# z projections of a mixer moved behind the Fourier inputs and kept in DRAM, with the Fourier branch beside the state steps

## Chip, cores and metric

The kernel runs on one core of one Trainium2 chip. The metric is the device time of one execution in microseconds, the median over several runs. The profile comes from one further execution, recorded by the hardware profiler; all times inside it count from its first instruction.

## What is computed

The program is a model of two blocks on 512 tokens of 1024 features. The first block has two layers of four attention branches with a feed-forward part. The second is one layer: modulation, a mixer, and a convolutional feed-forward part. The change is in the mixer. Cut to what matters, with `h` the modulated input:

```python
p = h @ w_in                                  # u, q, k, v, z and the gates, side by side
qkv = silu(dwconv1d(p[..., o1:o2], conv))     # three taps along the tokens; q and k to unit length
o, _, _ = bidir_gdn(q, k, v, beta, g, s_f, s_b)   # gated delta rule, forward scan + backward scan
y_f = fft2(u, axes=(tokens, group channels), norm='ortho').real @ w_f    # 4 groups of 128 features
y_d = rmsnorm_2(o, g_gdn) * silu(z)           # 4 heads of 128
y = concatenate([y_f, y_d]) @ w_out
x = x + gate * rmsnorm_2(y, g_post_mix)
```

One chunk of the delta rule, in each direction, needs the inverse of a triangular matrix I + A of its tokens (independent of the state), and then a step `v_new = u - w S`, `o = q S + attn v_new`, `S = S * decay + k^T v_new`.

## The kernel before

Values are held as pairs of float32r parts, high and low, and a product is three matmuls (L230 to L232). A weight block of 128x512 is loaded in fp32 by SP's DMA queue into `raw` (three buffers), cast by ScalarE to `whi` (L206), and its low part `wlo` is made by VectorE (L209) or GpSimd (L211), alternately; where `lo_pool` is true, always by GpSimd. A scheduler orders each engine's instructions, so that the order on an engine isn't that of the code.

The mixer's main part (the function that is printed below) works on four chunks of 128 tokens, four heads and two directions. In the order of the code:

- k, q and the gates; A of all chunks; the inverses of chunks 0 and 3, then of 1 and 2. An inverse begins with a substitution inside blocks of 16 tokens (L1174 shuffles, L1178 products, L1179 additions), whose second pair runs on VectorE with the products of one half (`own`) on GpSimd. It ends in `T` (L1189), which TensorE transposes (`tu`, L1200) and combines (`xp`, `up`).
- the Fourier inputs `us` (four projections of 128x512), q k^T for the steps (`gdn_attn`), the V projections with their convolution (`gdn_v`), and the Fourier matrix of each group, `Mg`.
- eight state steps, `gdn_step`: for each of four chunks both directions. On TensorE: `ks`, `qs`, `vp`, `av`, `sp`, 40 passes of 128x128. On VectorE: `S` and `r` from PSUM, `vd`, and `osum` or `ot`.
- `fourier`: first `between()`, the z projections (`proj_tm`, 192 matmuls of 128x256, eight weight blocks of `w2z`), then per group of features `V = u Mg` (16 matmuls) and 24 products `mm<-h,V` with the position matrix, and `yf` from them. z is evicted from PSUM by a tanh on ScalarE (`zt`, L1384) and one VectorE instruction (`zs`, L1385), which together give 2 silu(z); GpSimd multiplies it by the norm's gain (L1391).
- the gate of each chunk in the order 1, 0, 2, 3: the root mean square of `o` by small VectorE instructions on 128x4 elements (`ov`, `rq_i`, `rq_y`, `rq_t`, `of`), `oy` on VectorE (L1406), `oy` times `zs` on GpSimd (L1407), transposes `yt`, and the split `Yd`. Behind it the output projection `out_mix` and the sum of squares `ss` (L304).

The scheduler already places the 192 z matmuls partly between the steps: 150 of them stand in the steps and 42 behind them. The last `sp` of the steps ends near 2648.7 us.

Of the kernel before, what the change touches and what calls it, by code (L numbers as in the profile page):

```python
# [32 lines left out]
# ---------------------------------------------------------------- layout on the host  # L33
# [35 lines left out]
def pack(inp):  # L69
# [49 lines left out]
    # constants that depend on shapes alone  # L119
# [53 lines left out]
# ---------------------------------------------------------------- the program  # L173

class Prog:
# [12 lines left out]
    def side(self, shape, name):  # L188
        """Scratch of the work that runs beside a chain, which must not wait for the chain's own."""
        return self.wk.tile(shape, F32, name=name, tag="side", bufs=3)  # L190
# [5 lines left out]
    # ---- weights: fp32 as loaded -> an exact pair of float32r parts  # L196
# [17 lines left out]
    def blocks(self, src, nk, width=128, step=4):  # L214
        """Weights [128, nk * width], a pair of parts for each of the nk k-tiles."""
# [31 lines left out]
    # ---- 1/sqrt on the vector engine: shifted-exponent seed and three Newton steps  # L247
# [15 lines left out]
    # ---- 1/rms of each token over the features (on partitions), on every partition  # L263
# [24 lines left out]
    def rms_half(self, xs, scale=1.0 / D):  # L288
        """As rms, of half of the tokens."""
# [24 lines left out]
    def rms2(self, xs, gf):  # L314
        """For y = gain * x / rms(x): 1 / (rms(x) rms(y)) and 1 / rms(x) of each token, on every partition."""
# [55 lines left out]
    def setup_late(self):  # L371
        """Constants behind the first loads of x."""
# [17 lines left out]
    # ---- block 1  # L390
    def gain_split(self, xs, gcol):
        """Parts of x * gain, before the tokens' own factors 1 / rms are known."""
# [9 lines left out]
    def rms_row(self, xs, bank="t", tmp=None):  # L402
        """1 / rms of each token: along the free axis on every partition, and by token block."""
# [37 lines left out]
    def stack(self, t, z, i):  # L441
        """Parts of a head's 64 rows of z: rounded on its own rows of t, the rest on the other rows."""
        a, b = slice(i * 64, i * 64 + 64), slice(64 - i * 64, 128 - i * 64)
        self.nc.scalar.copy(t[a], z[a])
        self.nc.vector.tensor_sub(t[b], z[a], t[a])

    def score(self, s, q, k, a, stop):
        """q^T k in three products of parts; q stacked, k: parts of the keys on both halves of the rows."""
# [3 lines left out]
    def attn_head(self, h, score, add, diag, v, Y):  # L452
        """One causal head. v(b): parts of the values of key block b, side by side; Y: parts of the outputs."""
# [68 lines left out]
    def layer(self, l, xs):  # L522
# [23 lines left out]
        # -- indexer of branch B  # L546
# [21 lines left out]
        # -- branch A  # L568
# [31 lines left out]
        def pick(m, rounds=range(16)):  # L600
            """The 128 largest of each row become 0, the others NEG."""
# [48 lines left out]
        # -- branch B  # L650
# [16 lines left out]
        # -- branch C  # L667
# [28 lines left out]
        # -- branch D  # L696
# [20 lines left out]
        # -- out  # L717
# [194 lines left out]
    # ---- block 2  # L912
    def ada_steps(self):
        """Rows of the modulation's weights times silu(c), and for the first two also times silu(c_ctx)."""
# [67 lines left out]
    def gdn_k(self, G, H, n, between=None):  # L982
        """k: conv, silu, unit length; on tokens (G.ktm) and on features (G.kT)."""
# [73 lines left out]
    def gdn_gates(self, G, H, n):  # L1057
        """Beta, cumulated log decays and their exponentials (tokens on partitions)."""
# [37 lines left out]
    def gdn_a(self, G, cs):  # L1096
        """A of both directions of some chunks (before the triangle is cut out), and the decay."""
# [27 lines left out]
    def gdn_inv(self, G, cs, own=None):  # L1125
        """The inverse of I + A, transposed, columns of beta."""
# [16 lines left out]
    def tinv(self, G, As, own):  # L1143
        """Transposed inverses of I + A: by substitution within blocks of 16 tokens, then by pairs of blocks."""
        nc, n = self.nc, len(As)
        tl = lambda nm, shape: G.pool.tile(shape, F32, name=nm, tag=G.tags[nm][0], bufs=G.tags[nm][1])
        # the blocks' coefficients, columns in the order of the substitution
# [98 lines left out]
    def gdn_step(self, G, c, dr, S0, first):  # L1246
        """One chunk of one direction; S0: state before it (None: zero); returns the state after it."""
# [48 lines left out]
    def ctx_part(self, spool, mp):  # L1296
        """States of both directions after the context."""
# [29 lines left out]
    def mixer(self, xs, st, spool, mp):  # L1327
# [26 lines left out]
        for g in range(4):  # L1354
            nc.scalar.copy(us[g], self.proj(H, A["w2fm"][12 + g], S))
        self.lo_pool = False
# [293 lines left out]
```

## Time and profile before

| | before |
|---|---|
| median of 3 runs | 3150.69 us (3146.12 to 3153.24) |
| span of the profiled execution | 3146.6 us |
| mean granted TensorE clock | 0.976 |
| TensorE busy | 3005.7 us (96%) |
| VectorE busy | 2022.1 us (64%) |
| ScalarE busy | 1294.6 us (41%) |
| GpSimd busy | 853.4 us (27%) |

The span, from the first to the last instruction, is the only time shown for the profiled execution; the median lies 4.1 us above it. A busy share is an average over stages with different limits. What concerns the change lies between 2480 and 2720 us of the span.

### The profile page before, as it was taken

The page shows a single profiled execution, that of the slowest core. Times are in us where ns is not written, and L with a number is a line of the kernel's source. Part 1 is how long each engine was busy: PE and PEld are TensorE (multiplying, and loading weights), DVE is VectorE, ACT ScalarE, POOL GpSimd, SP SyncE. Part 2 cuts the span into 40 slices and gives each one's busy share as a digit, 9 for nine tenths or more (in the row PEclk, how much of TensorE's full clock was granted, in tenths as well). Part 3 has the DMA queues.
Part 4 walks back from the last instruction along what each step waited for, and adds up shares of the span by engine and source line. Part 5 has one row for each costly group of instructions (what it writes and reads, how often), then busy time and mean ns, then how long its engine had stood idle before and what let it go on. Part 6 is the DMA issues. An engine that isn't in the chain of part 4 may idle for free. (4 is left out here: it accounts for less than half of the span.)

```text
span 3146.6 us, 45203 instructions
## 1 busy us (share of the span) xinstructions
PE 3005.7 (96%) x16264; PEld 2496.3 (79%) x16264; DVE 2022.1 (64%) x4085; ACT 1294.6 (41%) x2601; POOL 853.4 (27%) x682
## 2 busy tenths in 40 slices
PE   8999999999999989999989999889999899899998
PEld 7767877788877868678877887778886689898997
DVE  5977264434978887874373436775466856785684
ACT  4355323334433333464233334533344533543332
POOL 2222324132222222113232332211221412422223
PEclk9999999999999989999999999999999999999998
DMA  3211312133344562112211233321332101323223
GB/s 124 70 37 44 101 57 89 44 111 131 111 151 161 173 190 81 38 41 74 94 61 61 93 123 97 102 61 65 96 91 96 60 23 53 116 67 93 98 85 110
DMA packets 152143, 280.97 MB, mean 89 GB/s; under 512 B 17520, under 2 KB 30192, under 8 KB 151792
## 3 DMA queue, kind: packets, MB, share of 16 engines
q1 hardware_dynamic: 146160, 266.93, 26.5%
q10 hardware_dynamic: 5472, 10.11, 1.0%
q8 instruction: 128, 2.10, 0.3%
q0 software_dynamic: 288, 1.05, 0.1%
q14 instruction: 95, 0.78, 0.1%
HBM read 271.74 MB, written 6.29 MB: 88 GB/s over the span
## 5 line engine op out<-in xcount | busy, mean ns | idle before, releaser
L211 POOL TENSOR_TENSOR wlo<-raw,whi 128x512 fp32r<-128x512 f32 (+3 forms) x446 | 597.6, 1341 | 1747.1 <-ACT whi L206 1586.5
L206 ACT CAST whi<-raw 128x512 fp32r<-128x512 f32 (+2 forms) x884 | 534.8, 608 | 998.1 <-PE mm L231 791.1
L230 PE MATMUL mm<-hhi,whi 128*128 128x512 f32 (+1 forms) x2520 | 927.5, 368 | 10.0 <-ACT whi L206 7.0
L232 PE MATMUL mm<-hhi,wlo 128*128 128x512 f32 (+2 forms) x2520 | 927.0, 368 | 4.6 <-DVE wlo L209 4.3
L231 PE MATMUL mm<-hlo,whi 128*128 128x512 f32 (+1 forms) x2520 | 923.2, 366 | 0.0
L230 PEld LDWEIGHTS mm<-hhi,whi 128*128 128x128 f32 x2520 | 478.2, 190 | 87.5 <-ACT whi L206 7.0
L232 PEld LDWEIGHTS mm<-hhi,wlo 128*128 128x128 f32 (+1 forms) x2520 | 477.8, 190 | 84.8 <-DVE wlo L209 6.0
L231 PEld LDWEIGHTS mm<-hlo,whi 128*128 128x128 f32 x2520 | 477.7, 190 | 77.5 <-issue 2.0
L209 DVE TENSOR_TENSOR wlo<-raw,whi 128x512 fp32r<-128x512 f32 (+3 forms) x438 | 326.5, 746 | 234.4 <-ACT whi L206 228.0
L230 PE MATMUL mm<-fhi,whi 128*128 128x512 f32 (+1 forms) x560 | 217.3, 389 | 17.4 <-ACT fhi L244 17.4
L231 PE MATMUL mm<-flo,whi 128*128 128x512 f32 (+1 forms) x560 | 217.5, 388 | 0.0
L232 PE MATMUL mm<-fhi,wlo 128*128 128x512 f32 (+1 forms) x560 | 217.0, 387 | 0.0
L230 PE MATMUL mm<-whi,hhi 128*128 128x256 f32 (+2 forms) x512 | 147.0, 287 | 6.5 <-ACT vM L562 5.6
L232 PE MATMUL mm<-yhi,wlo 128*128 128x512 f32 x384 | 152.0, 396 | 0.0
L230 PE MATMUL mm<-yhi,whi 128*128 128x512 f32 x384 | 151.9, 396 | 0.0
L231 PE MATMUL mm<-ylo,whi 128*128 128x512 f32 x384 | 151.2, 394 | 0.0
L231 PE MATMUL mm<-wlo,hhi 128*128 128x256 f32 (+2 forms) x512 | 147.1, 287 | 2.0 <-POOL wlo L211 2.0
L232 PE MATMUL mm<-whi,hlo 128*128 128x256 f32 (+2 forms) x512 | 146.4, 286 | 0.0
L230 PEld LDWEIGHTS mm<-fhi,whi 128*128 128x128 f32 x560 | 107.4, 192 | 41.1 <-ACT fhi L244 19.9
L739 DVE TENSOR_TENSOR mt<-mm,rrow 128x512 f32<-128x512 f32 x64 | 44.3, 692 | 134.8 <-PE mm L232 134.8
L1545 DVE SCALAR_TENSOR_TENSOR cv<-mm,cdwc,cv 128x441 f32<-128x441 f32 (+2 forms) x176 | 120.4, 692 | 10.6 <-PE mm L231 6.6
L231 PEld LDWEIGHTS mm<-flo,whi 128*128 128x128 f32 x560 | 107.8, 192 | 22.5 <-DVE flo L245 1.0
(513 smaller groups left out, 4922.1 us busy)
## 6 DMA issues: line engine op xcount, KB each, us to landing
raw<-wfm SPq DMA_DIRECT2D x240, 256.0 KB, 2.7
raw<-wup SPq DMA_DIRECT2D x176, 256.0 KB, 2.8
ada<-wada SPq DMA_DIRECT2D x48, 512.0 KB, 3.9
raw<-w2up SPq DMA_DIRECT2D x88, 256.0 KB, 2.8
raw<-wbr SPq DMA_DIRECT2D x64, 256.0 KB, 2.8
raw<-wdn SPq DMA_DIRECT2D x64, 256.0 KB, 2.7
raw<-w2fm SPq DMA_DIRECT2D x48, 256.0 KB, 2.8
raw<-w2dn SPq DMA_DIRECT2D x48, 256.0 KB, 2.7
```

The source lines that it names most:

```text
L206: nc.scalar.copy(hi[:, :n], raw[:, :n])
L209: nc.vector.tensor_sub(lo[:, :n], raw[:, :n], hi[:, :n])
L211: nc.gpsimd.tensor_sub(lo[:, :n], raw[:, :n], hi[:, :n])
L230: mm(out, a[0], b[0], start=first, stop=False)
L231: mm(out, a[0], b[1], start=False, stop=False)
L232: mm(out, a[1], b[0], start=False, stop=last)
L739: nc.vector.tensor_mul(t, g, self.row)
L1545: nc.vector.scalar_tensor_tensor(c[:, ro, co], p[:, ri, ci], w(a, b), c[:, ro, co], op0=OP.mult, op1=OP.add)
```

## The change

The z projections are called right behind the Fourier inputs, while `lo_pool` is true. They are evicted by a plain copy on ScalarE and stored to a DRAM tensor in eight parts of 128x256. Two loads of 128x1024 bring them back behind the steps, and tanh and the product of silu are then done from SBUF on 128x512. `fourier` no longer calls anything first. Its first two groups use the common PSUM banks alone (`both` false), so that they can stand beside the steps. The two directions of a step come in the order 1, 0.

```diff
+        def evz(j, p, i):
+            t = self.side([128, 256], "zt")
+            nc.scalar.copy(t, p)
+            nc.sync.dma_start(self.zspill[:, j, i * 256:i * 256 + 256], t)
+        for i in range(2):
+            self.proj_tm(H, A["w2z"][i], 256, lambda j, p: evz(j, p, i))
         self.lo_pool = False
...
         for i in range(4):
-            for dr in range(2):
+            for dr in (1, 0):
                 c = (3 - i) if dr else i
...
             z = mp.tile([128, 2, S], F32, name="zs", tag="T", bufs=2)
+            nc.sync.dma_start(z, self.zspill[:, 2 * i:2 * i + 2, :])
             zs += [z[:, 0, :], z[:, 1, :]]
-
-        def ev(j, p, i):
-            t = self.side([128, 256], "zt")
-            nc.scalar.activation(t, p, AF.Tanh, scale=0.5)
-            nc.vector.scalar_tensor_tensor(zs[j][:, i * 256:i * 256 + 256], t, 1.0, p, op0=OP.add, op1=OP.mult)
-        Y = self.fourier(us, Mg, mp, lambda: [self.proj_tm(H, A["w2z"][i], 256, lambda j, p: ev(j, p, i))
-                                          for i in range(2)])
+        Y = self.fourier(us, Mg, mp)
         gg = self.rows2[:, 16:144]
-        for j in range(4):
+        for j in (1, 0, 2, 3):
+            t = self.side([128, S], "zt")
+            nc.scalar.activation(t, zs[j], AF.Tanh, scale=0.5)
+            nc.vector.scalar_tensor_tensor(zs[j], t, 1.0, zs[j], op0=OP.add, op1=OP.mult)
             z4 = zs[j].rearrange("p (h e) -> p h e", h=4)
             nc.gpsimd.tensor_mul(z4, z4, gg[:, None, :].to_broadcast([128, 4, 128]))
...
-    def fourier(self, us, Mg, mp, between):
+    def fourier(self, us, Mg, mp):
         nc, ps, A = self.nc, self.ps, self.A
-        between()
-        self.both = True
...
         for g in range(4):
+            self.both = g > 1
...
+        P.zspill = nc.dram_tensor("zs", [128, 4, S], F32, kind="Internal").ap()
```

What this does to the order on the engines is shown at three places. The first is TensorE at the wait for `T` of the second pair of chunks. Before, V matmuls of 128x512 (output `mm`, inputs `hhi` and `hlo` from the left) stand ahead of it:

```order
L230 MATMUL mm_23104<-hhi_21529,whi_23113 128x512
L231 MATMUL mm_23104<-hlo_21530,whi_23113 128x512
L232 MATMUL mm_23104<-hhi_21529,wlo_23114 128x512
L1200 MATMUL tu_22351<-tri_98,T_22344 128x128 x4
L1200 MATMUL tu_22357<-tri_98,T_22344 128x128 x4
L1216 MATMUL xp_22376<-U_22350,A_21917 128x64
L1200 MATMUL tu_22364<-tri_98,T_22347 128x128 x4
```

Now the matmuls ahead of it are the z projections, of 128x256, weights from the left:

```order
L232 MATMUL mm_23139<-whi_23039,hlo_21512 128x256
L230 MATMUL mm_23139<-whi_23039,hhi_21511 128x256
L231 MATMUL mm_23139<-wlo_23040,hhi_21511 128x256
L1200 MATMUL tu_22351<-tri_98,T_22344 128x128 x4
L232 MATMUL mm_23139<-whi_23039,hlo_21512 128x256
L1200 MATMUL tu_22357<-tri_98,T_22344 128x128 x4
L230 MATMUL mm_23139<-whi_23045,hhi_21529 128x256
L1200 MATMUL tu_22364<-tri_98,T_22347 128x128 x4
```

The 48 V matmuls went behind `T`, and 83 z matmuls took the place; the other 109 z matmuls follow between `T` and the first step. The second place is TensorE in the seventh state step, from `qs` on. Before, z matmuls fill it:

```order
L232 MATMUL mm<-whi,hlo 128x256
L1263 MATMUL vp<-r,U 128x128
L230 MATMUL mm<-whi,hhi 128x256
L1263 MATMUL vp<-r,U 128x128
L231 MATMUL mm<-wlo,hhi 128x256
L1263 MATMUL vp<-r,U 128x128
L232 MATMUL mm<-whi,hlo 128x256
L1263 MATMUL vp<-r,U 128x128
L230 MATMUL mm<-whi,hhi 128x256
L231 MATMUL mm<-wlo,hhi 128x256
L232 MATMUL mm<-whi,hlo 128x256
L230 MATMUL mm<-whi,hhi 128x256
```

Now, from the seventh `ks` to the first products of the eighth step, one Fourier product and the `Mg,u` matmuls are left in the seventh, and none in the eighth:

```order
L1255 MATMUL ks<-S,kTx 128x128 x4
L1271 MATMUL qs<-S,qTx 128x128 x4
L232 MATMUL mm<-hhi,V 128x258
L1435 MATMUL mm<-Mg,u 128x128 x4
L1263 MATMUL vp<-r,U 128x128 x4
L1287 MATMUL sp<-vd,ktmx 128x128 x3
L1274 MATMUL av<-vn,attn 128x128 x4
L1287 MATMUL sp<-vd,ktmx 128x128
L1255 MATMUL ks<-S,kTx 128x128 x4
L1271 MATMUL qs<-S,qTx 128x128 x4
L1263 MATMUL vp<-r,U 128x128 x4
L1287 MATMUL sp<-vd,ktmx 128x128 x3
```

All other steps but the first have parts of the Fourier branch as well: 51 matmuls of `h,V` and the `Mg,u` matmuls of three groups, the rest of it following the last step. The third place is GpSimd from the end of the steps to the gate's first products `oy`. Before (L1391 is z times the gain, L1424 the low part of the position matrix):

```order
L1284 TENSOR_TENSOR osum<-osum,ot 128x512
L1391 TENSOR_TENSOR zs<-zs,rows_257 128x512
L1424 TENSOR_TENSOR hlo<-raw,hhi 128x512 x3
L1407 TENSOR_TENSOR oy<-oy,zs 128x512
L1391 TENSOR_TENSOR zs<-zs,rows_257 128x512
L1424 TENSOR_TENSOR hlo<-raw,hhi 128x512
L211 TENSOR_TENSOR wkeep<-raw,wkeep 128x512 x4
L1407 TENSOR_TENSOR oy<-oy,zs 128x512
```

Now (L1396 is z times the gain, L1412 `oy` times z):

```order
L1427 TENSOR_TENSOR hlo<-raw,hhi 128x512 x4
L1284 TENSOR_TENSOR osum<-osum,ot 128x512 x3
L211 TENSOR_TENSOR wkeep<-raw,wkeep 128x512 x2
L1284 TENSOR_TENSOR osum<-osum,ot 128x512
L211 TENSOR_TENSOR wkeep<-raw,wkeep 128x512 x2
L211 TENSOR_TENSOR wlo<-raw,whi 128x512
L1396 TENSOR_TENSOR zs<-zs,rows_257 128x512 x4
L211 TENSOR_TENSOR wlo<-raw,whi 128x512
L1412 TENSOR_TENSOR oy<-oy,zs 128x512
```

The four products of z, which stood beside the steps and between the first `oy`, now stand behind the steps in one piece; the low parts of the position matrix moved ahead of the last `osum`.

## Rows read from the trace of the kernel before

**Rows 1.** Table by stretch: window, length; PE, PEld, DVE, ACT, POOL busy; clock.

```profile
2499.10:2513.40 14.30, 0.47 (x3) 0.03 (x1) 13.76 (x58) 1.96 (x4) 6.04 (x7) 0.70 0.23 74
2513.40:2580.66 67.26, 67.24 (x572) 61.46 (x573) 37.65 (x83) 22.33 (x43) 15.94 (x16) 0.96 0.04 14
2580.66:2605.32 24.66, 22.74 (x140) 19.95 (x139) 10.58 (x35) 7.54 (x14) 0.00 (x0) 0.79 0.11 36
2605.32:2648.73 43.41, 43.41 (x376) 43.01 (x375) 26.37 (x85) 11.17 (x22) 8.96 (x7) 1.00 0.06 19
2648.73:2718.25 69.52, 55.10 (x421) 53.70 (x420) 54.65 (x120) 42.24 (x119) 32.72 (x26) 0.93 0.45 144
```

**Rows 2.** Timeline of TensorE around the wait for T: start, us.

```profile
2496.64 0.40 PE L230 MATMUL mm<-hhi,whi 128*128 128x512 f32 x1
...
2499.17 0.40 PE L232 MATMUL mm<-hhi,wlo 128*128 128x512 f32 x1
2513.42 1.52 PE L1200 MATMUL tu<-tri,T 128*128 128x128 f32 x5 [13.85 <-DVE T L1189]
```

**Rows 3.** Timeline of VectorE along the substitution chain.

```profile
2483.61 0.41 DVE L1178 TENSOR_TENSOR sb<-sb,ac 128x256 f32<-128x256 f32 x1
...
2492.52 0.41 DVE L1178 TENSOR_TENSOR sb<-sb,ac 128x256 f32<-128x256 f32 x1
...
2495.95 0.41 DVE L1178 TENSOR_TENSOR sb<-sb,ac 128x256 f32<-128x256 f32 x1
...
2498.28 0.42 DVE L1178 TENSOR_TENSOR sb<-sb,ac 128x256 f32<-128x256 f32 x1
...
2512.69 2.92 DVE L1189 TENSOR_TENSOR T<-tc,sub 128x512 f32<-128x512 f32 x4
```

**Rows 4.** Timeline of GpSimd in the same stretch.

```profile
2494.45 1.29 POOL L211 TENSOR_TENSOR wlo<-raw,whi 128x512 fp32r<-128x512 f32 x1
```

**Rows 5.** Timeline of TensorE within one state step.

```profile
2621.57 0.28 PE L230 MATMUL mm<-whi,hhi 128*128 128x256 f32 x1
2621.69 0.28 PE L231 MATMUL mm<-wlo,hhi 128*128 128x256 f32 x1
```

**Rows 6.** Timeline of VectorE within one state step.

```profile
2619.87 0.60 DVE L1293 SCALAR_TENSOR_TENSOR S<-S,eglx,sp 128x128 f32<-128x128 f32 x2 [2.14 <-PE sp L1287]
...
2621.94 1.12 DVE L1258 SCALAR_TENSOR_TENSOR r<-ks,ngcx,vtmx 128x128 f32<-128x128 f32 x4
...
2624.20 0.69 DVE L1265 TENSOR_TENSOR vd<-vp,edlx 128x512 f32<-128x512 f32 x1 [0.53 <-PE vp L1263]
...
2627.04 0.61 DVE L1293 SCALAR_TENSOR_TENSOR S<-S,eglx,sp 128x128 f32<-128x128 f32 x2
```

**Rows 7.** Groups of instructions, VectorE, 2648.73:2718.25: busy, mean ns, idle before.

```profile
L209 DVE TENSOR_TENSOR wlo<-raw,whi 128x512 fp32r<-128x512 f32 x7 | 5.9, 842 | 4.9 <-ACT whi L206 4.9
...
L245 DVE TENSOR_TENSOR V<-mm,V 128x256 fp32r<-128x256 f32 x16 | 5.9, 412 | 0.0
...
L245 DVE TENSOR_TENSOR hlo<-yf,hhi 128x512 fp32r<-128x512 f32 x4 | 2.8, 688 | 0.2
```

**Rows 8.** Timeline of VectorE in the tail.

```profile
2651.87 1.22 DVE L251 TENSOR_SCALAR rq_i<-ov 128x4 int32<-128x4 int32 x1
...
2656.83 0.16 DVE L259 SCALAR_TENSOR_TENSOR rq_y<-rq_t,rq_y 128x4 f32<-128x4 f32 x1
...
2698.57 0.69 DVE L1406 TENSOR_TENSOR oy<-osum,of 128x512 f32<-128x512 f32 x1
```

**Rows 9.** Timeline of TensorE in the tail.

```profile
2659.64 0.55 PE L230 MATMUL mm<-hhi,V 128*128 128x258 f32 x1 [4.20 <-DVE zs L1385]
...
2700.78 0.66 PE L1410 MATMUL yt<-tri,oy 128*128 128x128 f32 x4 [1.35 <-POOL oy L1407]
...
2718.25 0.91 PE L304 MATMUL ss<-tri,sq 128*128 128x1 f32 x7 [3.27 <-DVE sq L298]
```

**Rows 10.** Transfers issued in 2400:2720: engine, count, size, median us to landing.

```profile
raw<-w2fm SPq DMA_DIRECT2D x25, 256.0 KB, 2.8
```

## Prediction

> **What bounds the kernel now.** I read the mixer's stages from the table by stretch first [rows 1]. TensorE is full in 2513.4:2580.66 and 2605.32:2648.73, nearly full in 2580.66:2605.32 (22.74 of 24.66 us), and not full in two places: 2499.1:2513.4, where it did 0.47 us of work, and 2648.73:2718.25, 55.10 of 69.52 us with VectorE at 54.65. Only these can give time for nothing; work moved out of a full stretch into another full one changes nothing.
>
> The first hole: the timeline of TensorE shows the last V matmul at 2499.17 and then 13.85 us of idling until `tu` at 2513.42, which waited for VectorE's `T` [rows 2]. `T` stands at the end of the substitution chain (L1174 to L1179), which hops between VectorE and GpSimd: eleven rounds from 2483.61 to 2512.69 [rows 3]. A round without other work is 2.33 us (2495.95 to 2498.28). A round in which GpSimd also makes the low part of a weight block (1.29 us at 2494.45, [rows 4]) is 3.43 us (2492.52 to 2495.95), 1.1 more.
>
> The steps: TensorE packs z matmuls (0.12 us apart, [rows 5]) between a step's own. Two steps are 7.17 us apart by their first `S` (2619.87 and 2627.04, [rows 6]), all of it TensorE work [rows 1]. VectorE idles 2.14 us for `sp` and 0.53 us for `vp` in it.
>
> The tail behind the last `sp` (2648.73): the gate of each 128-token chunk is a chain of small VectorE instructions, `oy`, a product on GpSimd, and the transposes `yt`; the fourth `oy` comes at 2698.57, 49.84 us in [rows 8], its `yt` at 2700.78, and the root mean square's `ss` at 2718.25 [rows 9]. VectorE sets this: it has no gap to speak of up to there, and much of its time is not work. `rq_i` of 4 elements takes 1.22 us at 2651.87, while the same sort of instruction takes 0.16 at 2656.83 [rows 8]; in between GpSimd ran its low parts. I count from the timeline about 31.6 us of own work, 15 of instructions held like that, and 3.6 idle: an estimate, summed over the short rows.
>
> **The change, part by part.**
>
> *Ahead of `T`.* In before, 48 V matmuls stand there (0.23 us each: 2496.64 to 2499.17 is eleven of them, [rows 2]). In the new order 83 z matmuls do (first order piece), 83 x 0.12 = 9.8 us instead of 48 x 0.23 = 11.2 us. So the hole, which was left 13.85 us long, is filled a little less. `T` itself: VectorE loses its four low parts and one convolution product in the chain, GpSimd gets five low parts between its rounds where it had four. Eleven rounds with five at 3.43 and the rest at 2.33 to 2.45 give 28.0 to 28.7 us against 29.08 now [rows 3]; a `T` earlier by 1 us, or later by 1 if a low part that waits for its cast holds the next round as well. I take no change, with 1.5 us both ways.
>
> *Between `T` and the first step.* All 96 V matmuls now come here, 48 more than before: 48 x 0.2325 = 11.2 us. So do the other 109 of the 192 z matmuls, none of which was here: 109 x 0.118 = 12.9 us. This stretch had 67.24 of 67.26 us busy [rows 1], so nothing there hides them: **+24.0 us** for the start of the first step.
>
> *The steps.* They give up 150 z matmuls (17.7 us) and take 51 matmuls of `h,V` at the same 0.118 and 48 passes of `Mg,u` at 0.11 to 0.12, 11.9 us together. But a step can't get shorter than its own chain: `S` to the end of `r` 3.1 us, `vp` 0.45, `vd` 0.69, `sp` and the way back 2.14 [rows 6], with small gaps 6.5 us. The third step, with 21 Fourier matmuls, keeps 6.95 us; the five behind it sit at 6.5 to 6.8 whatever is in them (the seventh has hardly any fill, the eighth none: second order piece). 6.95 + 5 x 6.65 = 40.2 against 43.4 [rows 1]: -3.2. The first two are held by the convolution's and the norm's waits and lose some ten z matmuls: -1. Sum **-4.2 us**; bounds: 0 (the low parts of the Fourier matrix on GpSimd hold VectorE in them) and -7 (no slack at all).
>
> *The direction order* swaps which of two independent states goes first; each step has the same instructions, and the gate starts with chunk 1 in both. Nothing for it.
>
> *The tail.* TensorE's load falls by the 42 z matmuls and the Fourier part that moved, to about 38 us. What ends it is VectorE. Up to the fourth `oy` it loses 10 of 16 `V`, 4 of 8 `yf`, 2 of 4 `hlo` and two z products, by [rows 7] 16 x 0.41 (`V`; the other two kinds read PSUM at the same size) + 2 x 0.69 = 8.0 us; it gains four silu products of 128x512, for which the nearest rows are an unheld low part or `hlo` of the same size, 0.69, and two more low parts: 4.2 us. Back to back these rows overlap by some tenth, so I take -3.4 instead of -3.8. GpSimd has 17 instructions of 1.28 us in that stretch in both orders, so I keep the 15 us of holding. The fourth `oy` then comes 46.4 us behind the last `sp`. Behind it stood 2.2 us to `yt`, 114 matmuls (13.4), `yt` itself and the 3.27 us wait of `ss` [rows 9]; now 50 matmuls stand there (5.9): `ss` at 46.4 + 11.8 = 58.2 instead of 69.52. **-11.3 us.** Bounds: if each silu product is held a full 1.1 us more by GpSimd's products behind one another (third order piece), -7; if all holding went, -28 (below).
>
> The Trainium skill ("SBUF — State Buffer", section "SBUF: two separate sides") says that a VectorE instruction with two SBUF inputs and a GpSimd instruction exclude each other for their whole length. The 0.16 against 1.22 us of `rq_i` agree with it. Against this change it says that silu, which read PSUM, now reads SBUF twice and can be held: by that the tail would lose 4 x 1.1 = 4.4 us more and the sum below be +13.
>
> *The DRAM trip of z.* Eight stores and two loads go on SP's queue, between the weights of V. A weight block takes 2.8 us from issue to landing [rows 10]; the loads back are needed some 90 us later than the stores. Nothing for the data; for what waits behind a store, see the third rival.
>
> Sum: +24.0 - 4.2 - 11.3 = **+8.5 us**. The profiled execution's span is 3146.6, so 3155 for its like; the median of the runs is 4.1 above the span, and the forecast is 3150.7 + 8.5 = **3159 us**, 0.27% slower. A measurement of this kernel tells 0.2% (6.3 us) from no change.
>
> **Rivals.**
> 1. *The tail becomes TensorE's: faster.* If the holding goes with the z products that GpSimd made there, VectorE has under 30 us to the fourth `oy`, and TensorE ends last: 38.2 us of work + 3.3 = 41.5 instead of 69.5, -28. Sum -8.2: 3142 us. It decides from the point where the stretch falls under 49.7 us (the fourth `oy` at 38 instead of 46.4). For it: the two-cause picture of [rows 1], in which neither engine is full. Against: GpSimd's rows don't get fewer. The skill's "Perfetto Trace Analysis", section "Optimization Strategy", says that interleaving regimes with different busiest engines may pay; the steps (VectorE 26 of 43 us) and the Fourier stage are such a pair, and by the rule this rival would be the likeliest.
> 2. *No measurable change, about 3151.* `T` 2.5 us earlier because VectorE is rid of low parts, steps at -6, the tail at -14: sum +1 to +2. Each is within the bounds above, but all three have to come together.
> 3. *The queue.* A z store waits at the head of SP's queue until its block is evicted, and weight blocks of V stand behind it. If three of the groups come too late by one landing less what the three raw buffers cover, some 1.5 us each, it costs 4 to 5 us: 3164. Against it: 109 z matmuls lie between.
> 4. *The clock.* TensorE's granted clock was 0.70 in the hole and 0.79 in the first two steps, where it idled, and 0.96 to 1.00 where it was full [rows 1]; at 2659.64, after 4.20 us of idling, matmuls ran at the lower level (1.2 GHz). The new last steps and the tail are thinner. If the last two steps' own 9 us double in part and another 20 matmuls of the tail too, +8 to +10: 3168.
>
> **From cases to numbers.** My forecast has 0.42 (3153 to 3166 by its bounds); rival 1 has 0.20, rival 2 has 0.20, rivals 3 and 4 have 0.18 together. The forecast's edge within 0.2% gives 0.03 to no change: faster 0.20, same 0.23, slower 0.57. The range 3143 to 3171 leaves out about half of rival 1 and the ends of 4.
>
> **What would show it.** Right: `tu` of the second pair starts within 1.5 us of 2513.4 after an idle wait over 12 us; the first `ks` of the steps near 2604.7; steps 3 to 8 in 39 to 41 us; last `sp` near 2668.5; fourth `oy` 44 to 49 us behind it, `ss` near 2727. Wrong: the hole ahead of `tu` under 10 us; a tail under 50 us with TensorE waiting for nothing; TensorE waiting for casts of V weights.

## The result

The changed kernel is slower: 3168.94 us in the median of six runs (3155.50 to 3176.22) against 3149.28 us for the kernel before, a ratio of 1.0063 (95% interval 1.0045 to 1.0082); measured once more it was 1.0076 (1.0063 to 1.0088), 3170.12 against 3147.39 us. So the change costs about 20 to 23 us. (One of the 18 executions of before behind the second ratio, 3302.46 us at a granted clock of 0.838, is left out of it.) The profiled execution was the quickest of the changed kernel's first six, 3155.50 us with a span of 3153.6, and it ran the identical work ahead of the mixer in less time than the profiled execution of before. The groups of the decay product `gr`, well ahead of the first changed instruction, show it; from its view by tile, first of before, then of the changed kernel (duration, first and last start):

```profile
L1110 PE MATMUL gr<-tri,gcx x32: 272/273/323, 2451.2 to 2461.2; 128*128 128x128 f32 x32
```

```profile
L1110 PE MATMUL gr<-tri,gcx x32: 272/273/323, 2445.3 to 2455.3; 128*128 128x128 f32 x32
```

The changed execution is 5.9 us ahead there, for a reason that lies outside the change (in the changed kernel's second trace, further down, `gr` starts at 2452.92). I therefore measure each stage of all kernels from the first `gr` of the same execution. The table by stretch of the changed kernel answers to [rows 1]:

```profile
2499.80:2507.78 7.98, 0.47 (x5) 0.27 (x4) 6.78 (x38) 0.58 (x1) 2.42 (x4) 0.83 0.05 17
2507.78:2598.68 90.90, 90.47 (x730) 83.58 (x731) 40.50 (x81) 30.67 (x59) 23.97 (x22) 0.98 0.17 52
2598.68:2625.19 26.51, 23.34 (x139) 20.38 (x138) 10.84 (x33) 9.31 (x18) 2.71 (x3) 0.74 0.21 64
2625.19:2668.00 42.81, 39.76 (x324) 38.39 (x323) 30.29 (x97) 13.47 (x29) 5.65 (x4) 0.97 0.06 17
2668.00:2728.09 60.09, 47.88 (x285) 44.22 (x283) 50.28 (x104) 33.30 (x96) 30.78 (x23) 0.77 0.41 133
```

The full stretch from `T` to the first step grew from 67.24 to 90.9 us, and it is as full as it was. The steps (the third and fourth line) take about what they took. The tail is some 10 us shorter, and emptier: TensorE has 47.88 us in it where it had 55.10, at a granted clock of 0.77. TensorE's timeline shows the ends of these stages, as [rows 2] and [rows 9] did:

```profile
2483.62 0.39 PE L231 MATMUL mm<-wlo,hhi 128*128 128x256 f32 x1 [0.24 <-POOL wlo L211]
...
2487.12 0.39 PE L231 MATMUL mm<-wlo,hhi 128*128 128x256 f32 x1 [2.51 <-POOL wlo L211]
...
2490.61 0.58 PE L231 MATMUL mm<-wlo,hhi 128*128 128x256 f32 x1 [2.50 <-POOL wlo L211]
...
2507.78 1.11 PE L1200 MATMUL tu<-tri,T 128*128 128x128 f32 x4 [7.51 <-DVE T L1189]
...
2598.68 1.06 PE L1255 MATMUL ks<-S,kTx 128*128 128x128 f32 x8
...
2719.91 1.02 PE L1415 MATMUL yt<-tri,oy 128*128 128x128 f32 x4 [2.01 <-POOL oy L1412]
...
2728.09 1.02 PE L304 MATMUL ss<-tri,sq 128*128 128x1 f32 x8
```

The wait for `T` is 7.51 us instead of 13.85, but the z matmuls ahead of it wait for GpSimd's low parts, 5.25 us in three pieces: the hole has been broken up, not filled. On VectorE, the first round, `T`, the last `S`, the products of silu and the fourth `oy`, as [rows 3] and [rows 8] showed them:

```profile
2477.70 0.41 DVE L1178 TENSOR_TENSOR sb<-sb,ac 128x256 f32<-128x256 f32 x1
...
2507.04 5.09 DVE L1189 TENSOR_TENSOR T<-tc,sub 128x512 f32<-128x512 f32 x4
...
2668.47 0.61 DVE L1293 SCALAR_TENSOR_TENSOR S<-S,eglx,sp 128x128 f32<-128x128 f32 x2 [2.59 <-PE sp L1287]
...
2682.48 0.68 DVE L1394 SCALAR_TENSOR_TENSOR zs<-zt,zs 128x512 f32<-128x512 f32 x1
...
2684.98 2.97 DVE L1394 SCALAR_TENSOR_TENSOR zs<-zt,zs 128x512 f32<-128x512 f32 x3
...
2717.70 0.69 DVE L1411 TENSOR_TENSOR oy<-osum,of 128x512 f32<-128x512 f32 x1
```

The chain to `T` takes 29.34 us (2477.70 to 2507.04) against 29.08. Stage by stage, against before (all from the timelines). The eighth step ends with four `S`, in two pairs; "the last `S`" is here in every kernel the start of the first pair, which follows the last `sp`: 2648.73 us in before, as in the prediction, 2668.47 in the first trace of the changed kernel and 2683.21 in its second:

| | before | first trace of the changed kernel | second trace | forecast change |
|---|---|---|---|---|
| `gr` to `tu` | 62.26 | 62.48 (+0.2) | 61.74 (-0.5) | 0 |
| `gr` to the first `ks` | 129.50 | 153.38 (+23.9) | 163.13 (+33.6) | +24.0 |
| first `ks` to the last `S` | 68.07 | 69.79 (+1.7) | 67.16 (-0.9) | -4.2 |
| last `S` to `ss` | 69.52 | 59.62 (-9.9) | 60.08 (-9.4) | -11.3 |
| of which to the fourth `oy` | 49.84 | 49.23 (-0.6) | 50.25 (+0.4) | -3.4 |
| and from there to `ss` | 19.68 | 10.39 (-9.3) | 9.83 (-9.9) | -7.9 |
| `gr` to `ss` | 267.09 | 282.79 (+15.7) | 290.37 (+23.3) | +8.5 |

In the first trace +15.7 here, -5.9 ahead of it and -2.9 behind it give the span's +7.0. The second trace is of an execution of 3172.19 us; its +23.3 is as much as the difference of the medians. The whole gain of the tail lies behind the fourth `oy`, which comes no sooner than before: there TensorE has 50 matmuls left between the last `yt` and `ss`, where it had 114.

### The profile page after: what moved, and what is told of

It reads as the page before. It is cut to its first block, busy times and chain, and to the rows that moved or that the text cites. A ratio compares the mean times of both kernels' runs of the same rounds, so it can differ in the third digit from the quotient of the medians.

```text
span 3153.6 us, 45222 instructions
## 1 busy us (share of the span) xinstructions
PE 3011.1 (95%) x16264; PEld 2499.1 (79%) x16264; DVE 2022.4 (64%) x4077; ACT 1296.2 (41%) x2605; POOL 859.7 (27%) x686
## 4 chain that ended last, share of the span: by engine, by line
PE 48%; DVE 9%; ACT 2%; issue 2%; DMA 1%; POOL 1%; POOLq 0%; ACTq 0%; SPq 0%; DVEq 0%
PE mm L230 12%; PE mm L231 12%; PE mm L232 12%; PE s L642 1%; DVE wlo L209 1%; PE xp L1216 1%; PE up L1225 1%; PE pt L483 1%; PE tu L1200 1%; DVE M L605 1%; PE s L450 0%; DVE m L604 0%; ACT whi L206 0%; DVE rq_y L259 0%; PE yp L487 0%
```

## The experiments

All were timed against the kernel before on the same chip, and profiled. They were made in four sets; the theory at the start was that of the prediction.

**Once more** (the changed kernel without an edit).

> The changed kernel once more. In the first pair of traces the executions stood 5.9 us apart before the changed part begins (first decay product gr at 2451.2 before, 2445.3 after). Theory (the move costs 24 us ahead of the steps, the steps give nothing back, the tail gives 10): measured from gr, T stays within 1 us, the first ks comes 24 us later, the sum of squares ss 15 to 16 us later, and the median is 14 to 20 us over before. Rival (TensorE's clock in thinner stretches decides): the stretch from gr to ss changes by more than 4 us between this trace and the first one of the changed kernel.

3170.12 us, 1.0076 (1.0063 to 1.0088). The stretch from `gr` to `ss` took 290.37 us, 7.6 more than in the first trace: past the theory's 15 to 16 and past the rival's 4. The rival's sign came, then, but not where a stretch is thin. The whole of the difference, and more, lies between `T` and the first step, where TensorE is full: the first `ks` comes 9.75 us later, and the steps take 2.6 us less than in the first trace. Here are two stretches behind `tu`, 12.6 and 13 us long, of the first trace and then of this one (clock third from the end):

```profile
2507.70:2520.30 12.60, 12.09 (x93) 11.82 (x93) 9.35 (x24) 3.51 (x7) 5.60 (x6) 0.84 0.13 43
2520.30:2533.30 13.00, 13.00 (x124) 12.36 (x123) 7.31 (x18) 4.96 (x10) 2.19 (x3) 1.00 0.00 1
```

```profile
2515.32:2527.92 12.60, 12.18 (x59) 11.91 (x57) 7.09 (x16) 2.83 (x5) 4.20 (x4) 0.50 0.14 43
2527.92:2540.92 13.00, 13.00 (x65) 13.00 (x64) 4.09 (x16) 2.35 (x4) 1.28 (x2) 0.51 0.00 0
```

TensorE is busy in both, and does 124 matmuls in this trace where it did 217 in the first: the granted clock is 0.50, the 1.2 GHz level, for 26 us behind the wait of 6.82 us for `T`, where the first trace and before were back at 1.00 within 13. That is where the 9.75 us at the first `ks` arise. The table by stretch of this trace for the first two steps, the other six and the tail, and on VectorE the last `S`:

```profile
2616.05:2641.30 25.25, 22.19 (x138) 19.33 (x137) 10.77 (x33) 9.31 (x18) 2.69 (x3) 0.80 0.21 64
2641.30:2683.21 41.91, 38.86 (x327) 37.50 (x326) 30.31 (x97) 13.48 (x29) 5.65 (x4) 1.00 0.05 14
2683.21:2743.29 60.08, 43.13 (x281) 39.70 (x280) 50.13 (x104) 33.42 (x96) 30.33 (x24) 0.86 0.42 138
```

```profile
2683.21 0.61 DVE L1293 SCALAR_TENSOR_TENSOR S<-S,eglx,sp 128x128 f32<-128x128 f32 x2 [1.22 <-PE sp L1287]
```

In the first trace the last step's `sp` ran at the lower level and the step took 8.25 us; here it ran at 1.00 and the step took 6.88.

**Directions alone.**

```diff
-            for dr in range(2):
+            for dr in (1, 0):
```

> The kernel before with the two directions of a step in the order 1, 0 and nothing else. Theory: the same within 3 us, steps 68 us, tail 69.5 us. Rival (the order of the directions delays chunk 1, which the gate takes first): the first oy comes later by a step's part, 3 to 7 us, and the time rises by as much.

3148.35 us, 1.0003 (0.9993 to 1.0013): no difference. `gr` to `ss` is 266.32 us, and the first `oy` comes at 2659.88 us, 9.7 us behind the last `S`, as before. This part of the change is worth nothing.

**The Fourier branch behind the steps again.**

```diff
-            self.both = g > 1
+            self.both = True
```

> The changed kernel with all four Fourier groups on both sets of PSUM banks, so that all but some 10 matmuls of the Fourier branch stand behind the steps and steps 3 to 8 have no fill. Theory (a step cannot get shorter than its own chain): steps 3 to 8 still take 39 to 41 us, against 43.3 with the fill, and the tail gets 4 to 10 us longer because VectorE has 10 more V and 4 more yf there: 1 to 7 us over the changed kernel. Rival clock: TensorE drops to its lower level in steps that it fills by two thirds, steps 3 to 8 take 46 us or more, and the time rises by 10 us or more. Rival fill: the steps shrink by the whole of their fill, to 33 us.

3172.33 us, 1.0089 (1.0075 to 1.0103). It is the cleanest look at a step's own chain. The third step, with hardly any fill, and the fourth, with none, from TensorE's timeline:

```profile
2631.74 1.06 PE L1255 MATMUL ks<-S,kTx 128*128 128x128 f32 x8
2636.46 0.94 PE L1287 MATMUL sp<-vd,ktmx 128*128 128x128 f32 x6 [0.78 <-DVE vd L1265]
...
2638.35 1.06 PE L1255 MATMUL ks<-S,kTx 128*128 128x128 f32 x8
2643.07 1.51 PE L1287 MATMUL sp<-vd,ktmx 128*128 128x128 f32 x6 [0.78 <-DVE vd L1265]
...
2646.51 1.13 PE L1255 MATMUL ks<-S,kTx 128*128 128x128 f32 x8
```

6.61 us for the one, 8.16 for the next, in whose `sp` the clock drops; the others are 6.65, 6.61, 6.68 and, up to the last `S`, 6.89. The floor of 6.5 that the prediction put together from one step's rows holds. The six together:

```profile
2631.74:2673.34 41.60, 32.89 (x248) 30.60 (x247) 25.22 (x84) 9.05 (x16) 5.63 (x4) 0.96 0.02 6
```

41.6 us is 0.6 over the theory's 41, by the one step that lost 1.5 us to the clock, and far from the clock rival's 46 and the fill rival's 33. With the fill (the Fourier matmuls that stand between a step's own) steps 3 to 7 take 6.68 to 7.49 us in the first trace of the changed kernel ([rows 6] for before: 7.17), so a step is little longer. The tail is 67.7 us, 8.1 longer than in that trace, `gr` to `ss` 4.5 longer, and the median 2 to 3 us over the changed kernel's; tail and median are inside the forecast.

**z behind V.** The call of the z projections moves behind `gdn_v`:

```diff
-        for i in range(2):
-            self.proj_tm(H, A["w2z"][i], 256, lambda j, p: evz(j, p, i))
         self.lo_pool = False
...
         self.gdn_v(G, H, S)
+        for i in range(2):
+            self.proj_tm(H, A["w2z"][i], 256, lambda j, p: evz(j, p, i))
```

> The changed kernel with the z projections called behind the V projections: V fills the hole ahead of T as before, and all 192 z matmuls fall into the first state step, where TensorE idled about 2 us. Theory (only the place of TensorE's work counts, and the full stretch has to take z in any case): 1 to 4 us faster than the changed kernel, 11 to 15 us slower than before by the mixer's part. Rival queue (the z stores delay the V weights on SP's queue): with the stores behind all V weights the gain over the changed kernel is 5 to 10 us.

3153.33 us, 1.0019 (1.0009 to 1.0030): 17 us better than the changed kernel, four times what I expected and more than the queue rival's 10. `gr` to the first `ks` is 129.39 us, as before. The table by stretch, of the first step and then of the second, whose `ks` is spread (cut where its last part starts):

```profile
2579.30:2608.69 29.39, 27.77 (x230) 27.04 (x229) 5.64 (x10) 9.41 (x20) 5.68 (x5) 1.00 0.32 98
2608.69:2613.22 4.53, 3.52 (x20) 2.41 (x19) 2.04 (x8) 2.42 (x5) 2.22 (x2) 1.00 0.91 297
2613.22:2622.24 9.02, 9.02 (x69) 9.01 (x68) 3.57 (x11) 3.12 (x6) 0.00 (x0) 0.84 0.23 67
```

Without their 192 x 0.118 = 22.7 us of z matmuls, the steps take 85.2 - 22.7 = 62.5 us, 7.3 and 4.6 less than in the two traces of the changed kernel. The gain lies in the first two steps, which wait for VectorE and ScalarE in any case (26.51 and 25.25 us in the changed kernel, 42.9 - 22.7 = 20.2 here), and with z standing in the first the clock is at 1.00 through most of them, where it was 0.74 and 0.80. So two things were mixed in this gain, the stretch behind `T` and the first steps. The second set takes them apart.

**z's low parts on both engines.**

```diff
+        self.lo_pool = False
         def evz(j, p, i):
```

> The changed kernel with the low parts of the z weights made by VectorE and GpSimd alternately instead of GpSimd alone. The trace of the changed kernel shows TensorE waiting for GpSimd's low parts three times (0.24, 2.51, 2.50 us) ahead of the 7.5 us wait for T, and in the second execution its clock stayed at the lower level for 26 us behind that. Theory (the broken wait ahead of T is what leaves the clock low): 96 instead of 83 z matmuls stand ahead of T, the waits for low parts go, T moves by 1 us at most, the first ks comes 150 to 153 us behind gr (163 in the second execution), and the median is 11 to 16 us over before. Rival (the low clock has nothing to do with these waits): 20 to 24 us over before as it was.

3158.67 us (3157.69 to 3162.85), 1.0037 (1.0025 to 1.0049): about 11 us better than the changed kernel and 10.5 over before, at the lower edge of the theory's 11 to 16; the rival's 20 to 24 falls. The first `ks` comes 151.68 us behind `gr`, and the clock is back at 1.00 within 13 us of `tu`. `T` moved by 0.8 us. But the waits of TensorE ahead of `tu`, which I had expected to go, did not:

```profile
2496.34 0.39 PE L231 MATMUL mm<-wlo,hhi 128*128 128x256 f32 x1 [1.88 <-DVE wlo L209]
...
2500.18 0.58 PE L231 MATMUL mm<-wlo,hhi 128*128 128x256 f32 x1 [2.87 <-POOL wlo L211]
...
2518.97 1.11 PE L1200 MATMUL tu<-tri,T 128*128 128x128 f32 x4 [7.19 <-DVE T L1189]
```

A broken wait alone did not leave the clock low in this execution, then, and the theory's reason does not hold, though its times do.

**z between the V projections.** `gdn_v` calls z behind its second projection:

```diff
+                if h == 1 and mid:
+                    mid()
```

> The changed kernel with the z projections called between the second and the third V projection: two V projections fill the wait for T as before, and all z stands in the full stretch between T and the first step, none in the first step. It splits what the kernel with z behind V won (17 us by its median). Theory (two parts: some 10 us from the clock behind the wait for T, some 7 from the first steps, whose waits z filled there): first ks 152 us behind gr, steps 69 to 71 us, tail 59, 12 to 16 us over before. Rival (all of the gain came from the first steps): 20 us or more over before. Second rival (all from the wait for T): 8 us or less over before.

3161.32 us (3155.36 to 3162.18), 1.0037 (1.0025 to 1.0049), 13 us over before and inside the theory's 12 to 16. V fills the hole much as before (10 z matmuls stand ahead of `tu`, which waits 10.82 us), and the rest of z stands in the full stretch: first `ks` 150.66 us behind `gr`, steps 66.1 (three less than expected), tail 61.6. Both rivals fall. Together with the experiment before it: z ahead of the steps costs some 12 us in all, once the tail's gain is taken off, with z or with V in the hole; the low clock behind `T` costs another 10; and placing z inside the first step, not ahead of it, gains 5 to 7.

**Stores doubled.**

```diff
             nc.sync.dma_start(self.zspill[:, j, i * 256:i * 256 + 256], t)
+            nc.sync.dma_start(self.zspare[:, j, i * 256:i * 256 + 256], t)
```

> The changed kernel with each of the eight z stores issued twice, the second to a DRAM tensor that nothing reads: the cost of the stores on SP's queue, doubled. Theory (the queue is not in the way): within 4 us of the changed kernel, TensorE waits for no V weights. Rival queue (the stores delay the weights of V): 4 to 10 us more, with waits of TensorE for casts between T and the first step.

3172.19 us, 1.0070 (1.0050 to 1.0090), 24 us over before, where the changed kernel was 20 and 23 over. Between `T` and the first step TensorE waits for no weight. The queue is not in the way. The clock behind `T` was at the lower level in this trace too (0.50 and 0.53 in the two stretches that were shown above).

**Silu and gain where z is evicted** (on the kernel with z behind V):

```diff
-            nc.scalar.copy(t, p)
...
+            nc.scalar.activation(t, p, AF.Tanh, scale=0.5)
+            nc.vector.scalar_tensor_tensor(u, t, 1.0, p, op0=OP.add, op1=OP.mult)
...
+            nc.gpsimd.tensor_mul(t, t, self.rows2[:, None, 16:144].to_broadcast([128, 2, 128]))
...
-            nc.scalar.activation(t, zs[j], AF.Tanh, scale=0.5)
-            nc.vector.scalar_tensor_tensor(zs[j], t, 1.0, zs[j], op0=OP.add, op1=OP.mult)
...
-            nc.gpsimd.tensor_mul(z4, z4, gg[:, None, :].to_broadcast([128, 4, 128]))
```

> The kernel with z behind V, and silu and the gain applied where z is evicted, beside the first step: tanh and the product from PSUM in parts of 128x256, the gain on GpSimd, then the store; the tail has neither silu nor gain any more. Theory (VectorE sets the tail, much of it held by GpSimd): without four silu products (2.8 us) and four GpSimd products (5.1 us, each of which can hold VectorE) the fourth oy comes 40 to 45 us behind the last S instead of 49.5, ss 50 to 55 instead of 59.4, and the time is 5 to 9 us under the kernel with z behind V, which is 0 to 3 us under before. Rival (TensorE sets the tail): within 2 us of the kernel with z behind V.

3155.08 us, 1.0019 (1.0010 to 1.0028): no gain over the kernel with z behind V, though the tail did what was expected. So the rival's time came, but not for its reason. The fourth `oy` and `ss`, behind a last `S` at 2669.60 (VectorE, then TensorE):

```profile
2709.62 0.69 DVE L1408 TENSOR_TENSOR oy<-osum,of 128x512 f32<-128x512 f32 x1
```

```profile
2721.43 1.02 PE L304 MATMUL ss<-tri,sq 128*128 128x1 f32 x8
```

40.0 and 51.8 us, 7.6 us less tail. The steps gave it back: 92.3 us from the first `ks` to the last `S`, 7.0 more than the 85.2 of the kernel with z behind V. The first two steps:

```profile
2577.35:2615.24 37.89, 32.13 (x242) 29.58 (x241) 9.12 (x18) 12.86 (x26) 13.76 (x14) 0.95 0.38 119
2615.24:2626.80 11.56, 11.56 (x91) 11.54 (x90) 6.21 (x25) 3.20 (x8) 0.00 (x0) 0.85 0.13 41
```

They were 42.9 us there and are 49.4 here. In the order all `vp` stand behind the z matmuls, where there six of the first step's eight stood ahead; TensorE's waits in the two steps are 5.8 us instead of 2.6, and the clock of the first is 0.95 instead of 1.00.

**The same with `Mg` ahead of z.**

```diff
-        for i in range(2):
-            self.proj_tm(H, A["w2z"][i], 256, lambda j, p: evz(j, p, i))
         G.o = [None] * 4
...
             nc.scalar.activation(Mg[:, i], p, AF.Copy, scale=1.0 / 256)
+        for i in range(2):
+            self.proj_tm(H, A["w2z"][i], 256, lambda j, p: evz(j, p, i))
```

> As the kernel with silu and gain at the eviction of z (z behind V), with the Fourier matrix Mg and its loads ahead of z, so that the first step waits neither for that load (1.75 us in the trace) nor for Mg behind z, and the Fourier branch starts earlier beside the steps. Theory (what is left over before is waiting and the lower clock in the first two steps, 49.5 us from the first ks to the third against 22.7 of z matmuls and some 17 of their own): the two steps take 42 to 46 us, the tail 51 to 53, ss comes 267 to 271 us behind gr, and the time is 2 us under to 4 us over before. Rival (the first step waits for its own chain whatever stands before it): no change against the kernel before this one, 5 to 7 us over before.

3159.48 us, 1.0038 (1.0024 to 1.0053). The first two steps take 50.4 us by their first `ks` on TensorE:

```profile
2580.52 1.06 PE L1255 MATMUL ks<-S,kTx 128*128 128x128 f32 x8
...
2624.32 1.06 PE L1255 MATMUL ks<-S,kTx 128*128 128x128 f32 x8
...
2630.95 1.06 PE L1255 MATMUL ks<-S,kTx 128*128 128x128 f32 x8
```

Not 42 to 46; the load of `dc` is waited for all the same (1.54 us). In the steps the rival holds (50.4 us against 49.4), but the time, 10 us over before, lies outside its 5 to 7 as well as outside the theory. The tail, 52.6 us, is as expected; `ss` comes 276.9 us behind `gr`, not 267 to 271.

**The gate's small instructions in pairs of chunks**, on three kernels: mean square, reciprocal root and factor of chunks 1 and 2, then of 0 and 3, as 128x8 instead of four times 128x4.

```diff
-        for c in (1, 0, 2, 3):
+        for p in ((1, 2), (0, 3)):
...
-            r = self.rsqrt(v, [128, 4])
+            r = self.rsqrt(v, [128, 8])
...
+        for c in (1, 2, 0, 3):
```

> The kernel before with the gate's small VectorE instructions done for two chunks at once, 1 with 2 and 0 with 3 (128x8 instead of 128x4; the first pair is complete after the sixth step), so half as many. Theory (the tail is set by VectorE, and its small instructions, 21 us in 69.5, many of them held, are the largest part): the fourth oy comes 35 to 42 us behind the last S instead of 49.8, ss 58 to 63 instead of 69.5, limited by TensorE's 55 us of work there; 7 to 12 us faster than before. Rival (transfers or weight casts set the tail): less than 3 us.

On the kernel before: 3147.86 us, 0.9996 (0.9984 to 1.0008), no difference. In the trace the fourth `oy` comes at 2682.42, 33.9 us behind the last `S` (2648.52) instead of 49.8. But `ss` is only 1.45 us sooner. The tail's stretch, and TensorE's last `yt` and its `ss`:

```profile
2648.52:2716.59 68.07, 56.63 (x421) 53.88 (x420) 44.28 (x94) 42.10 (x119) 33.16 (x26) 0.92 0.47 147
```

```profile
2688.84 1.06 PE L1416 MATMUL yt<-tri,oy 128*128 128x128 f32 x4
...
2716.59 1.84 PE L304 MATMUL ss<-tri,sq 128*128 128x1 f32 x8 [3.21 <-DVE sq L298]
```

VectorE lost 10 of its 54.65 us and the end hardly moved. TensorE's own 56.63 us with its 11.4 us of waits end it now: 6.1 us ahead of Fourier matmuls, 3.2 for `ss`, and 2.1 for weight casts. The theory's 7 to 12 us did not come. The rival's "less than 3 us" came out, but weight casts are the smallest of these waits.

> The changed kernel with the same pairing. Theory: its tail is set by VectorE more than that of before, since TensorE has only some 38 us to do there at full clock; ss comes 46 to 52 us behind the last S instead of 56 to 60, 8 to 13 us faster than the changed kernel. All of the tail that the move could give would then be about 20 us, still less than the 24 us ahead of the steps: no faster than the paired kernel before. Rival (TensorE's low clock sets this tail): less than 4 us.

On the changed kernel: 3178.43 us, 1.0091 (1.0077 to 1.0105), 28 us over before, so 5 to 8 slower than the changed kernel instead of 8 to 13 faster. TensorE's timeline:

```profile
2700.20 1.12 PE L1421 MATMUL yt<-tri,oy 128*128 128x128 f32 x4 [6.75 <-POOL oy L1418]
2708.34 1.11 PE L1421 MATMUL yt<-tri,oy 128*128 128x128 f32 x4 [7.02 <-POOL oy L1418]
...
2746.05 1.35 PE L304 MATMUL ss<-tri,sq 128*128 128x1 f32 x8 [4.73 <-DVE sq L298]
```

The scheduler, for which `oy` is early now, puts the transposes of the first two chunks ahead of the 72 weight products that stood before them, and TensorE waits 13.8 us for them in place. `ss` comes 64.8 us behind the last `S`, with the clock at 0.79. The rival's "less than 4 us" does not fit either.

> The kernel with z behind V, with the same pairing. Theory: 8 to 13 us faster than the kernel with z behind V, so 2 to 7 us under before, and 3 to 8 us over the paired kernel before. Rival (once the tail is TensorE's, taking work out of it pays): faster than the paired kernel before.

On the kernel with z behind V: 3158.52 us, 1.0030 (1.0019 to 1.0041), 8 us over before, where it was 6 over without the pairing: no gain, and in the traces `gr` to `ss` is 7.0 us longer, with the same two waits (6.84 and 7.03 us). The theory fails, and so does the rival. None of the versions beats the kernel before.

## Why the prediction was right, and what it missed

**The time** came out at 3169 to 3170 us, slower as forecast, inside the range but 10 us above the predicted 3159. By the second trace the sum was +23.3 and not +8.5: 9.6 us were missing ahead of the first step, 3.3 in the steps and 1.9 in the tail.

**Ahead of `T`: no change in `T`** (0 forecast, +0.2 and -0.5 measured). The working doesn't give this: by its own prices eleven rounds, five at 3.43 us, are 31.1 to 31.9 us and not 28.0 to 28.7. In the first trace there are ten from the first round to the last, five of 3.17 to 3.53 us and five of 1.82 to 2.34, and 1.08 us from there to `T`. That z fills the hole "a little less" was too kind: the z matmuls are drawn out by GpSimd's low parts until 2499.8, so that the hole in all is 7.51 + 5.25 = 12.8 us against 13.85. The sign "an idle wait over 12 us" failed with it (7.51 and 6.82). It made no difference to the first step where the clock came back: 23.9 us in the first trace.

**+24.0 us for the first step**: shown. It is 23.9 in the first trace and again with the Fourier branch behind the steps, 22.2 and 21.2 in the two kernels of the second set that move z or its low parts, and nothing (-0.1) where z stands in the first step. Work that was put into this full stretch cost its whole length.

**Behind `T`** the forecast had no term, and this is the step that failed. "This stretch had 67.24 of 67.26 us busy" took it that a full stretch runs at full clock. The second trace, that with doubled stores and one of the paired kernels have the first `ks` 163 to 164 us behind `gr` instead of 153; in the second trace TensorE did 124 matmuls where the first had 217, in the same 26 us, which cost 9.75 us. Rival 4 priced the low clock in the steps and the tail, at +8 to +10, and not there. That its 3168 us stands beside the measured 3169 is luck: the size agrees, the place does not.

**The steps** were forecast to give 4.2 us; they took 1.7 in the first trace and gave 0.9 in the second. The floor was right (6.61 to 6.68 measured against 6.5). The term was mis-sized at two places. The third to eighth step take 41.9 us in the second trace, not 40.2: with fill they are 7.1, 7.0, 6.7, 7.5 and 6.7 us, the empty last one 6.9. In the first trace they take 43.3, because the last one is at the lower level and takes 8.25 us. And the first two take 26.5 and 25.3 us instead of 23.7, at a clock of 0.74 and 0.80. In the two kernels of the second set that move z or its low parts all steps take 67.7 and 66.1 us, so -0.4 and -2.0: half of the forecast at most.

**The tail** was forecast at -11.3 and gave -9.9 and -9.4. The sum came near by two misses that partly cancel. The fourth `oy` was to come 3.4 us sooner, 46.4 us behind the last `S`, and came at 49.2 and 50.2, as before (49.8), for VectorE's busy time up to it fell by 1.2 us only, from 44.7 to 43.4 and 43.5. Behind it `ss` was to take 11.8 us (12.1 by the prediction's own rows: 19.68 less 64 matmuls at 0.118) and took 10.4 and 9.8. So the tail got shorter because TensorE has less left behind the last `oy`: 64 fewer matmuls (7.5 us), and `ss`, which waited 3.27 us before, waits 1.04 us in the second trace and not at all in the first. The cause that the prediction gives, "what ends it is VectorE", does not hold as it stands. Where the fourth `oy` came 16 us sooner, before stayed the same, with TensorE as the bound, and the other two gained nothing, because the order on TensorE changed with it. Where silu and gain were taken out, the tail did shrink by 7.6 us.

**The rivals.** The first (a tail of TensorE alone, faster) fell with the tail at 60 us, the second (three small gains at once) with `T`, which did not move. The "Perfetto Trace Analysis" page of the Trainium skill, section "Optimization Strategy", which would have made it the likeliest, speaks of performance that may be improved; here the two regimes were indeed interleaved, steps and Fourier, and the steps gained 0.9 us at most in the two traces; that this is because z already stood in them is my reading. The third (the queue) fell with the doubled stores. As for the lock that the Trainium skill describes ("SBUF — State Buffer", section "SBUF: two separate sides"): one silu product took 0.68 us alone, and the three beside GpSimd's products took 2.97, so 3.65 us against 2.7 unheld. One of the three was held, 1.76 us long beside a GpSimd product that had started 0.45 us before it. The trace agrees in kind, at about 1 us and not the 4.4 that all four fully held would cost. The prediction's own pair for it was not a clean one: `rq_i`, 1.22 us, reads one tensor, and its 0.16 is another instruction's, `rq_y`.

**What stays open**: which execution gets the low clock behind `T`. In five traces TensorE's order is the same from `gr` to the first step. It recovered in the first trace and in that with the Fourier branch behind the steps, after a wait of 7.51 and 7.47 us for `T`, and not in the three others, after 6.82, 7.01 and 7.12; whether the length of the wait has to do with it no run shows. That z's place and its low parts decide how often it happens is suggested by the medians (about 11 us apart) and one trace of each kernel; what in them does it is not known. Of the 6.5 us that the first two steps lost with silu and gain where z is evicted, TensorE's waits explain 3.1; with `Mg` ahead of z as well, 1.9 of 7.5. The rest is not explained.

## To carry to other kernels

Before moving fill out of a stage, ask where it goes: here z was nearly free beside the steps, which were never shorter than 6.6 us each in any trace, while the move put 24 us of matmuls into the stretch ahead of them and took only 10 off the tail. Count the stretch behind a wait at TensorE's lower clock too, and not only at its work, and look at several executions, since one profile can be the kind one. And a chain that a profile shows busy to the end is the bound only for the order of instructions in that profile: shorten it, and a scheduler may put the waits somewhere worse. Last, take the ends of stages at the same instruction in every trace: here two pairs of `S` that end the last step lie 1.6 to 4.1 us apart, as much as the differences in question.

## What the runs showed that I had not expected

- TensorE stayed at its lower clock level (0.50) for 26 us behind a 6.8 us wait, busy in 25.2 of 25.6 us; in other executions of the same order of instructions it was back at 1.00 within 13 us. The difference at the first step is 9.75 us.
- A step without fill, in which TensorE is busy for 5.1 of 6.6 us, ran mostly at the full level; where the clock dropped inside it, it took 8.2 us.
- Fill in a waiting stage paid twice: with 192 z matmuls in the first step, the first two steps took 20.2 us beyond the z work and ran mostly at a clock of 1.00; without, 26.5 and 25.3 us at 0.74 and 0.80.
- Halving VectorE's chain in the tail of before brought the fourth `oy` 16 us forward and the end 1.5.
